# Reordering the start of a decoder step: x ahead of the constants, the first modulation's weights ahead of the projection's, TensorE's transposes of x spread

## The chip, the cores and the metric

The kernel runs on one core of one Trainium2 chip. A core has a matrix engine (TensorE, PE in the profile, with PEld for its weight loads), VectorE (DVE), ScalarE (ACT), GpSimd (POOL), and SyncE (SP), which here issues all transfers between device memory and the core's SBUF. Matmuls write into PSUM banks, from which DVE and ACT read. The metric is the device time of one execution in microseconds, the median of several runs.

## The reference, cut to what matters

One layer of a decoder for a prompt (512 tokens) and 8 x 8 sampled tokens, all in fp32. The part that the change concerns is the first three lines:

```
mod = einsum('bd,dn->bn', silu(c), w_ada) + b_ada
sh1, sc1, g1, sh2, sc2, g2 = split(mod, 6)
u = x * (1 + sc1) + sh1
proj = einsum('bsd,dn->bsn', u, w_in)      # 10752 columns: q, k, v, recurrence, gates
...                                        # attention, HGRN2 recurrence, branches, w_out,
...                                        # LayerNorm, squared-ReLU MLP, LayerNorm
```

c has 9 rows (one for the prompt, eight for the samples), x 576 rows of 1024. Only sh1 and sc1 are needed for u.

## The kernel before, in words

Everything lives with the model dimension on partitions: x is transposed on PE into eight tiles xT[k] of 128 x 576 (k counts the 128-wide slices of the 1024 columns), and u likewise. fp32 products are made of three passes of a faster type: each operand is cast to a high part on ACT (whi, uh) and the remainder is subtracted on DVE (wlo, ul), and a product is hi*hi + hi*lo + lo*hi. A projection block of 128 output columns over all k thus takes 8 x 3 matmuls for each half of the tokens.

Each engine works through its instructions in the order in which the Python code issues them; nothing is reordered at run time. Later in the kernel a planner (`Side`, with a cost model in `Engine`) mixes attention work between the projection's matmuls; the start, which the change concerns, is written out by hand, near the end of `decoder_step`.

The start has these parts:

- `x_load(e)` loads half e of x's columns as five tiles `xtm` (four of the prompt, one of the samples). `x_transposed(xtm, ks)` makes xT[k]: four transposes of 128 x 128 and one of 64 x 64 on PE into two PSUM banks tagged "tr", one copy on ACT, one on DVE.
- `ada_load(s)` loads the weights of modulation s (s = 0 to 3): eight tiles `wada`, 256 KB each. Set s holds the shift and the scale for k = 2s and 2s + 1.
- `ada(s, w)` is a generator in two halves. The first: eight matmuls (PE `tr<-wada,cT`, sixteen records in a trace) and a copy to SBUF on ACT (`moda`). The second: four transposes on PE (`tr<-ident,moda`), a reduction on DVE (`mt`), and an addition (`mod`). Each `next(shift[s])` runs one half.
- `make_u(k)` makes u for slice k: ACT writes uh for the prompt, POOL and ACT for the samples, DVE makes u and then the remainder ul.
- `load_one()` loads one slot of w_in: `wraw`, 1 MB, four slices of k and four blocks j. `split_slot(u0, j, slot)` makes whi and wlo of block j from it. Slot 0 serves k = 0 to 3, slot 1 k = 4 to 7.
- `early_mm(k)` makes the products of slice k for the first three blocks (`n_early`), each in two token halves, into the banks tagged lin, att and sx: 18 matmuls.

Before the change SP first issues ctile (the rows of c), ident (the identity), block_mask, vecs (all bias rows), then x's first half, slot 0 of w_in, two sets of modulation weights, x's second half, the third set, slot 1 of w_in, and the fourth set. PE transposes c and vecs, then x's columns 0 to 3, then runs the first modulation. After that, for each s: second half of modulation s, u for its two slices, the products of slice 2s - 1, those of slice 2s, the first half of modulation s + 1, and (for s = 0, 1) two more columns of x. In what follows "block 3" is the first projection block after this early stage; it is where the hand-written start ends.

Of the kernel before, what the change touches and what calls it, by code (L numbers as in the profile page):

```python
# [11 lines left out]
F32 = mybir.dt.float32  # L12
F32R = mybir.dt.float32r
U8 = mybir.dt.uint8
AF = mybir.ActivationFunctionType
OP = mybir.AluOpType
# [7 lines left out]
NS = NB * NTK  # L24
# [12 lines left out]
C_M0, C_M1, C_M2, C_SBC, C_SBN, C_BM, C_ID = 0, 256, 384, 512, 896, 1280, 1284  # L37
# [206 lines left out]
def decoder_step(ctx, tc, I, O):  # L244
# [21 lines left out]
    def page(shape, name, dtype=F32):  # L266
        return pages.tile(shape, dtype, name=name, tag="page")

    def bank(shape, tag, bufs=2):
        return psum.tile(shape, F32, name=tag, tag=tag, bufs=bufs)  # L270
# [9 lines left out]
    ident = consts.tile([128, 128], F32, name="ident")  # L280
    SP.dma_start(ident, I["cst"][:, C_ID:C_ID + 128])
    block_mask = consts.tile([128, 4], F32, name="block_mask")
    SP.dma_start(block_mask, I["cst"][:, C_BM:C_BM + 4])
    bias_of = {}
    vecs = page([128, 128], "vecs")
    SP.dma_start(vecs, I["rows"])
    lm = consts.tile([128, 8, 128], U8, name="lm")
# [89 lines left out]
    def split_slot(u, j, s):  # L377
        k0, kk, t = u["slots"][s]
        hi, lo = u["w"].setdefault(j, ([], []))
        for k in range(0, kk, 4):  # L380
            src = t[:, k:k + 4, j * 128:(j + 1) * 128]
            hi.append(page([128, 4, 128], "whi", F32R))
            lo.append(page([128, 4, 128], "wlo", F32R))
            A.activation(hi[-1], src, AF.Copy)
            V.tensor_sub(lo[-1], src, hi[-1])
# [88 lines left out]
    A.activation(csg, ctile, AF.Tanh, scale=0.5)  # L474
    V.scalar_tensor_tensor(csg, csg, 1.0, ctile, op0=OP.add, op1=OP.mult)
    V.tensor_scalar(csg, csg, 0.5, None, op0=OP.mult)
    pv = bank([128, 256], "tr")
    PE.transpose(pv[:, 128:200], csg, ident[:72, :72])
    PE.transpose(pv[:, 0:128], vecs, ident)
    V.tensor_copy(cT[:, :, 0:9], pv[:, 128:200].rearrange("p (k n) -> p k n", n=9))  # L480
    vT = consts.tile([128, 128], F32, name="vT")
    V.tensor_copy(vT, pv[:, 0:128])
    for part in (1, 4):
        V.tensor_scalar(vT[:, 8 * part:8 * part + 8], vT[:, 8 * part:8 * part + 8], 1.0, None, op0=OP.add)

    def vcol(off, k):
        return vT[:, off + k:off + k + 1]

    hnw = consts.tile([128, 1], F32, name="hnw")
    V.tensor_scalar(hnw, vcol(V_HN, 0), 0.5, None, op0=OP.mult)  # L490
    lbt = consts.tile([128, 4, 8], F32, name="lbt")
    lb0, lb1 = (vT[:, ROWS["lb_param"] + 8 * e:ROWS["lb_param"] + 8 * e + 8] for e in range(2))
    V.tensor_max(lbt[:, 0], lb0, lb1)
    V.tensor_sub(lbt[:, 1], lb0, lbt[:, 0])
    V.tensor_sub(lbt[:, 2], lb1, lbt[:, 0])
    A.activation(lbt[:, 1:3], lbt[:, 1:3], AF.Exp)
    V.tensor_add(lbt[:, 3], lbt[:, 1], lbt[:, 2])
    V.reciprocal(lbt[:, 3], lbt[:, 3])
    V.tensor_mul(lbt[:, 0], lbt[:, 1], lbt[:, 3])
    V.tensor_scalar(lbt[:, 1], lbt[:, 0], -0.5, 0.5, op0=OP.mult, op1=OP.add)  # L500
    V.tensor_scalar(lbt[:, 0], lbt[:, 0], 0.5, 0.5, op0=OP.mult, op1=OP.add)

    mod = consts.tile([128, 48, 9], F32, name="mod")

# [3 lines left out]
    def ada_load(s):  # L508

        wk = [page([128, 2, 256], "wada") for _ in range(KT)]  # L510
        for k in range(KT):
            src = I["w_ada"][0][k * 128:(k + 1) * 128, 0:2048].rearrange("p (a c) -> p a c", a=2)
            SP.dma_start(wk[k], src[:, :, s * 256:(s + 1) * 256])
        return [w.rearrange("p a c -> p (a c)") for w in wk]

    def ada(s, wk=None, u=None):

        if u:
            load_more()
            while not loaded(u):  # L520
                yield 0, 1000
                load_more()
            yield 0, tuple(t for _, _, t in u["slots"])
        pa = bank([128, 512], "sx" if u else "tr")
        for k in range(KT):
            PE.matmul(pa[32 * (k % 4):32 * (k % 4) + 32], cT[:, k], u["slots"][k // 4][2][:, k % 4] if u else wk[k],
                      start=(k < 4), stop=(k >= 4), skip_group_check=True)
        if u:
            weights_done(u["slots"])
        ma = page([128, 512], "moda")  # L530
        A.activation(ma, pa, AF.Copy)
        yield 1900, 2000.0
        pm = bank([128, 4, 128], "sx" if u else "tr")
        for jj in range(4):
            PE.transpose(pm[:, jj], ma[:, jj * 128:(jj + 1) * 128], ident)
        mt = tiny([128, 4, 9], "mt")
        V.tensor_reduce(mt, pm.rearrange("p j (q n) -> p j n q", q=4)[:, :, 0:9], axis=AX.X, op=OP.add)
        if u:
            m, b = mod[:, s * 4:s * 4 + 4], vT[:, s * 4:s * 4 + 4, None]
        else:  # L540
            m, b = (t.rearrange("p (a k) n -> p a k n", a=2)[:, :, 2 * s:2 * s + 2] for t in (mod[:, 0:16], vT[:, 0:16, None]))
            mt = mt.rearrange("p (a k) n -> p a k n", a=2)
        V.tensor_add(m, mt, b.to_broadcast(list(mt.shape)))
        if u and s in (4, 5):
            V.tensor_scalar(m, m, 0.5 / ALPHA, None, op0=OP.mult)
        yield 436, 0
# [961 lines left out]

    xT = []

    def x_load(e):
        ts = []
        for b in range(5):
            rows = 128 if b < 4 else NS
            t = page([128, 512], "xtm")
            src = I["x_prompt"][0, b * 128:(b + 1) * 128] if b < 4 else I["x_sample"].rearrange("b t d -> (b t) d")
            SP.dma_start(t[:rows], src[:, e * 512:(e + 1) * 512])
            ts.append(t)
        return ts

    def x_transposed(xtm, ks):
        for k in ks:
            c = slice(k * 128, (k + 1) * 128)
            t = page([128, NT], "xT")
            xT.append(t)
            xp = bank([128, 4, 128], "tr")
            for b in range(4):
                PE.transpose(xp[:, b], xtm[b][:, c], ident)
            A.activation(t[:, 0:NP], xp.rearrange("p a b -> p (a b)"), AF.Copy)
            xsp = bank([128, NS], "tr")  # L1530
            PE.transpose(xsp, xtm[4][0:64, c], ident[0:64, 0:64])
            V.tensor_copy(t[:, NP:NT], xsp)
# [6 lines left out]
    def ahead(i):  # L1539
        while i < len(flat):  # L1540
            u, j = flat[i]
            if "ada" in u:
                if id(u) not in done_split:
                    done_split.add(id(u))
                    side.add("a", ada(u["ada"], u=u))
                i += 1
                continue
            if (id(u), j) not in done_split and not (u["tok"] and j % 5):
                done_split.add((id(u), j))
                split(u, j)  # L1550
            return

    def make_u(k):

        t = page([128, NT], "u32")
        U_hi[k], U_lo[k] = page([128, NT], "uh", F32R), page([128, NT], "ul", F32R)
        x = xT[k]
        A.activation(U_hi[k][:, 0:NP], x[:, 0:NP], AF.Identity, scale=mcol(1, k), bias=mcol(0, k))
        G.tensor_mul(sm(t[:, NP:NT]), sm(x[:, NP:NT]), msam(1, k))
        G.tensor_add(sm(t[:, NP:NT]), sm(t[:, NP:NT]), msam(0, k))  # L1560
        V.tensor_scalar(t[:, 0:NP], x[:, 0:NP], mcol(1, k), mcol(0, k), op0=OP.mult, op1=OP.add)
        A.activation(U_hi[k][:, NP:NT], t[:, NP:NT], AF.Copy)
        V.tensor_sub(U_lo[k], t, U_hi[k])

    xs = [page([128, 4, 128], "xs", F32R) for _ in range(2)]

    xa = x_load(0)
    load_one()
    wa = [ada_load(0), ada_load(1)]
    xb = x_load(1)  # L1570
    wa.append(ada_load(2))
    load_one()
# [5 lines left out]
    n_early = 3  # L1578
    u0 = units[0]
    early = {}  # L1580

    def early_mm(k):
        for j in range(n_early):
            for h in range(2):
                if k == 0:
                    early[j, h] = bank([128, HF], ("lin", "att", "sx")[j])
                mm_part(u0["w"][j], 8, u_x, h, early[j, h], (k,))

    x_transposed(xa, range(4))
    for j in range(n_early):  # L1590
        done_split.add((id(u0), j))
        split_slot(u0, j, 0)
    shift = [ada(s, w) for s, w in enumerate(wa)]
    wa.clear()
    next(shift[0])
    for s in range(4):
        next(shift[s])
        for k in (2 * s, 2 * s + 1):
            make_u(k)
        if s == 3:  # L1600
            ahead(n_early)
        if s:
            early_mm(2 * s - 1)
        if s == 2:
            next(shift[3])
        early_mm(2 * s)
        if s < 2:
            next(shift[s + 1])
            x_transposed(xb, (2 * s, 2 * s + 1))
        if s == 1:  # L1610
            for j in range(n_early):
                split_slot(u0, j, 1)
    early_mm(KT - 1)
    shift.clear()
    for j in range(n_early):
# [729 lines left out]
```

## Time and profile before

| | us |
|---|---|
| median of 3 runs | 1359.46 (1358.33 to 1359.71) |
| the profiled execution | 1361.52 |
| its span, first to last instruction | 1359.7 |
| PE busy in the span | 1308.3 |
| first matmul of the first modulation | 16.65 |
| first product of the projection | 24.12 |
| block 3 begins | 59.73 |

A row of the profile names the engine, the operation, and the tiles as out<-in; a bracket behind it gives the idle time of the engine ahead of it and what ended that. The line is always L173, since a helper records every operation, so one reads by tiles. A granted clock of 1.00 is TensorE's full clock, 0.50 half of it. The record of the granted clock begins at 21.75 us; before that a view shows 1.00 for want of a record.

### The profile page before, as it was taken

The numbers are of one execution on the slowest core, as the hardware profiler recorded it, in microseconds if no ns is written. First come the engines' busy times: TensorE is split into PE (matmuls) and PEld (weight loads), VectorE is DVE, ScalarE is ACT, GpSimd is POOL, SyncE is SP. The second block draws the span as 40 slices with busy tenths as digits, with TensorE's granted clock in tenths as the row PEclk, the third lists the DMA queues.
The fourth block names the chain that finished last, engine by engine and source line by source line (L and its number), as shares of the span: only waits on it lengthen the run. The fifth ranks groups of instructions, "written<-read, shape, count | busy, mean of one in ns | idle before, by whom it ended". The sixth has DMA issues, their size and how long they took to land.

```text
span 1359.7 us, 24393 instructions
## 1 busy us (share of the span) xinstructions
PE 1308.3 (96%) x9480; PEld 1206.2 (89%) x9480; DVE 837.9 (62%) x1669; ACT 524.2 (39%) x1164; POOL 319.7 (24%) x367
## 2 busy tenths in 40 slices
PE   6999999999889899999999999999999999999996
PEld 3899899899878787788898999999899999999995
DVE  2446556557776886657555526656545744766867
ACT  2423323333332322333233423224555742753851
POOL 0332023016525673225234400000530000000004
PEclk9999999999999999999999999999999999999999
DMA  9789889789988887775545514241126352453522
GB/s 292 266 294 333 274 290 350 250 264 319 295 275 282 295 286 252 222 246 173 171 146 166 159 32 140 68 158 64 62 81 248 115 198 113 156 225 119 221 95 70
DMA packets 186824, 274.11 MB, mean 202 GB/s; under 512 B 16012, under 2 KB 92628, under 8 KB 186196
## 3 DMA queue, kind: packets, MB, share of 16 engines
q1 hardware_dynamic: 186708, 272.54, 59.7%
q8 instruction: 75, 1.23, 0.4%
q14 instruction: 41, 0.34, 0.1%
HBM read 212.81 MB, written 76.46 MB: 213 GB/s over the span
## 4 chain that ended last, share of the span: by engine, by line
PE 82%; DVE 7%; DMA 4%; ACT 3%; issue 2%; POOL 1%; SPq 0%; DVEq 0%; POOLq 0%; ACTq 0%
PE lin L173 60%; PE att L173 11%; PE sx L173 7%; PE tr L173 4%; DVE wlo L173 2%; DMA qb<-qsc 2%; DVE res L173 1%; DMA out_dram<-kv 1%; DMA sgl<-ssc 1%; ACT whi L173 1%; DVE sc L173 1%; DVE hf L173 0%; DMA xtm<-in_x_sample_dram 0%; DVE st L173 0%; SPq L173 0%
## 5 line engine op out<-in xcount | busy, mean ns | idle before, releaser
L173 DVE TENSOR_TENSOR wlo<-wraw,whi 128x512 fp32r<-128x512 f32 (+1 forms) x335 | 271.1, 847 | 107.5 <-ACT whi L173 104.5
L173 PE MATMUL lin<-uh,whi 128*128 128x288 f32 x992 | 298.5, 301 | 5.3 <-DVE hso L173 3.7
L173 PE MATMUL lin<-uh,wlo 128*128 128x288 f32 x992 | 298.8, 301 | 1.9 <-DVE wlo L173 1.9
L173 PE MATMUL lin<-ul,whi 128*128 128x288 f32 x992 | 299.0, 301 | 1.2 <-DVE ul L173 1.2
L173 ACT ACTIVATE whi<-wraw 128x512 fp32r<-128x512 f32 (+1 forms) x335 | 211.3, 681 | 111.2 <-PE lin L173 36.5
L173 PEld LDWEIGHTS lin<-ul,whi 128*128 128x128 f32 x992 | 187.7, 189 | 14.4 <-issue 11.6
L173 PEld LDWEIGHTS lin<-uh,whi 128*128 128x128 f32 x992 | 187.7, 189 | 11.2 <-DVE hso L173 4.2
L173 PEld LDWEIGHTS lin<-uh,wlo 128*128 128x128 f32 x992 | 187.7, 189 | 6.9 <-issue 3.8
L173 POOL TENSOR_TENSOR qb<-qb,kv 128x512 f32<-128x512 f32 x96 | 128.9, 1360 | 202.8 <-DMA qb<-qsc 69.6
L173 PE MATMUL lin<-hdl,whi 128*128 128x288 f32 (+1 forms) x448 | 133.3, 298 | 1.4 <-DVE hdl L173 1.4
L173 PE MATMUL lin<-hdh,whi 128*128 128x288 f32 (+1 forms) x448 | 134.1, 299 | 0.0
L173 PE MATMUL lin<-hdh,wlo 128*128 128x288 f32 (+1 forms) x448 | 133.2, 297 | 0.0
L173 POOL TENSOR_TENSOR res<-res,lgb 128x512 f32<-128x512 f32 (+2 forms) x10 | 14.8, 1484 | 335.8 <-ACT res L173 335.4
L173 PEld LDWEIGHTS lin<-hdl,whi 128*128 128x128 f32 x448 | 84.5, 189 | 1.7 <-DVE hdl L173 1.7
L173 PEld LDWEIGHTS lin<-hdh,whi 128*128 128x128 f32 x448 | 84.5, 189 | 0.0
L173 PEld LDWEIGHTS lin<-hdh,wlo 128*128 128x128 f32 x448 | 84.3, 188 | 0.0
L173 PE MATMUL lin<-whi,uh 128*128 128x512 f32 x160 | 69.6, 435 | 2.5 <-ACT whi L173 1.1
L173 PE MATMUL lin<-wlo,uh 128*128 128x512 f32 x160 | 64.8, 405 | 1.1 <-DVE wlo L173 1.1
L173 DVE TENSOR_REDUCE sc<-qb 128x4 f32<-128x512 f32 x96 | 63.6, 678 | 3.3 <-POOL qb L173 3.1
L173 PE MATMUL lin<-whi,ul 128*128 128x512 f32 x160 | 64.0, 400 | 0.0
L173 POOL TENSOR_TENSOR hk<-hk,T 128x256 f32<-128x256 f32 (+1 forms) x48 | 40.7, 847 | 71.7 <-PE att L173 43.2
L173 ACT ACTIVATE P<-P,stat_p 128x128 f32<-128x128 f32 (+1 forms) x48 | 20.1, 420 | 93.7 <-DVE stat_p L173 93.7
(427 smaller groups left out, 2893.5 us busy)
## 6 DMA issues: line engine op xcount, KB each, us to landing
wraw<-in_w_in_dram SPq DMA_DIRECT2D x42, 1024.0 KB
kv<-in_cache_kv_w_dram SPq DMA_DIRECT2D x144, 256.0 KB
qb<-qsc SPq DMA_DIRECT2D x96, 256.0 KB
wraw<-in_w_down_dram SPq DMA_DIRECT2D x18, 1024.0 KB
out_dram<-kv SPq DMA_DIRECT2D x64, 256.0 KB
wraw<-in_w_ada_dram SPq DMA_DIRECT2D x16, 1024.0 KB
wraw<-in_w_up_dram SPq DMA_DIRECT2D x16, 1024.0 KB
out_dram<-in_cache_kv_w_dram SPq DMA_DIRECT2D x32, 512.0 KB
```

The costliest lines, as they stand in the source:

```text
L173: return f(out, *args, **kw)
```

## The change

Four things move; no instruction's work changes.

1. On SP, block_mask and vecs go behind x's first half, and slot 0 of w_in goes behind the first set of modulation weights.
2. On PE, the transposes of x are spread: columns 0 and 1, then vecs, then the first half of modulation 0, then columns 2 and 3. The second half of x (columns 4 to 7) goes ahead of the first halves of modulations 2 and 3 instead of behind those of 1 and 2.
3. Six to twelve products of an odd slice are split off: some stand ahead of a modulation's second half, the rest behind it.
4. On ACT and DVE, the casts of slot 0 are issued between and behind `make_u(0)` and `make_u(1)`, the casts of slot 1 behind `make_u(4)` and `make_u(5)`, and the work on `lbt` (bounds of the recurrence's gate) goes from the very start into modulation 1.

The SP queue at its start, as a difference (- before, + now):

```order
 L173 DMA ctile<-in_c_rows_dram 72x128
 L173 DMA ident<-in_cst_dram 128x128
-L173 DMA block_mask<-in_cst_dram 128x4
-L173 DMA vecs<-in_rows_dram 128x128
 L173 DMA xtm<-in_x_prompt_dram 128x512 x4
 L173 DMA xtm<-in_x_sample_dram 64x512
-L173 DMA wraw<-in_w_in_dram 128x4x512
-L173 DMA wada<-in_w_ada_dram 128x2x256 x16
+L173 DMA vecs<-in_rows_dram 128x128
+L173 DMA wada<-in_w_ada_dram 128x2x256 x8
+L173 DMA wraw<-in_w_in_dram 128x4x512
+L173 DMA block_mask<-in_cst_dram 128x4
```

So x's five tiles are the third to seventh transfer instead of the fifth to ninth, and the first eight wada tiles no longer follow wraw.

On PE, modulation 1 of before, from its matmuls to the first product of the next slice:

```order
L173 MATMUL tr<-wada,cT 32x512 x8
L173 MATMUL tr<-ident,xtm 128x128 x4
L173 MATMUL tr<-ident,xtm 128x64
L173 MATMUL tr<-ident,xtm 128x128 x4
L173 MATMUL tr<-ident,xtm 128x64
L173 MATMUL tr<-ident,moda 128x128 x4
L173 MATMUL lin<-uh,whi 128x288
```

The same modulation now; the six sx products are the last of slice 1, and the lin product is the first of slice 2:

```order
L173 MATMUL tr<-wada,cT 32x512 x8
L173 MATMUL tr<-ident,moda 128x128 x4
L173 MATMUL sx<-uh,whi 128x288
L173 MATMUL sx<-ul,whi 128x288
L173 MATMUL sx<-uh,wlo 128x288
L173 MATMUL sx<-uh,whi 128x288
L173 MATMUL sx<-ul,whi 128x288
L173 MATMUL sx<-uh,wlo 128x288
L173 MATMUL lin<-uh,whi 128x288
```

The ten transposes of x have left the place between the two halves. In before the lin product shown belongs to slice 1, whose u was made earlier; all 18 products of slice 1 stand there.

On ACT, modulation 2 of before (the copy moda, x's columns 6 and 7, slot 1's casts, then u of slices 4 and 5):

```order
L173 ACTIVATE moda<-tr 128x512
L173 ACTIVATE xT<-tr 128x512 x2
L173 ACTIVATE whi<-wraw 128x512 x3
L173 ACTIVATE uh<-xT,mod 128x512
L173 ACTIVATE uh<-u_509 128x64
L173 ACTIVATE uh<-xT,mod 128x512
L173 ACTIVATE uh<-u_518 128x64
```

The same place now (xT is here columns 6 and 7 again):

```order
L173 ACTIVATE moda<-tr 128x512
L173 ACTIVATE uh<-xT,mod 128x512
L173 ACTIVATE uh<-u_484 128x64
L173 ACTIVATE uh<-xT,mod 128x512
L173 ACTIVATE uh<-u_493 128x64
L173 ACTIVATE whi<-wraw 128x512 x3
L173 ACTIVATE xT<-tr 128x512 x2
```

Slot 1's three casts stand behind both slices' u instead of ahead of them. The diff's core:

```diff
-    SP.dma_start(block_mask, I["cst"][:, C_BM:C_BM + 4])
...
+    xa = x_load(0)
     vecs = page([128, 128], "vecs")
     SP.dma_start(vecs, I["rows"])
...
-    xa = x_load(0)
+    wa = [ada_load(0)]
     load_one()
-    wa = [ada_load(0), ada_load(1)]
+    SP.dma_start(block_mask, I["cst"][:, C_BM:C_BM + 4])
+    wa.append(ada_load(1))
     xb = x_load(1)
...
-    def early_mm(k):
-        for j in range(n_early):
+    def early_mm(k, js=range(n_early)):
+        for j in js:
...
-    x_transposed(xa, range(4))
+    shift = [ada(s, w) for s, w in enumerate(wa)]
+    wa.clear()
+    x_transposed(xa, (0, 1))
+    vectors()
+    next(shift[0])
+    x_transposed(xa, (2, 3))
+    next(shift[0])
     for j in range(n_early):
         done_split.add((id(u0), j))
+        if j < 2:
+            make_u(j)
         split_slot(u0, j, 0)
-    shift = [ada(s, w) for s, w in enumerate(wa)]
-    wa.clear()
-    next(shift[0])
-    for s in range(4):
-        next(shift[s])
-        for k in (2 * s, 2 * s + 1):
-            make_u(k)
-        if s == 3:
-            ahead(n_early)
-        if s:
-            early_mm(2 * s - 1)
-        if s == 2:
-            next(shift[3])
-        early_mm(2 * s)
-        if s < 2:
-            next(shift[s + 1])
-            x_transposed(xb, (2 * s, 2 * s + 1))
-        if s == 1:
-            for j in range(n_early):
-                split_slot(u0, j, 1)
+    early_mm(0)
+    early_mm(1, (0, 1))
+    next(shift[1])
+    gate_bounds()
+    next(shift[1])
+    make_u(2)
+    make_u(3)
+    early_mm(1, (2,))
+    early_mm(2)
+    x_transposed(xb, (0, 1))
+    next(shift[2])
+    early_mm(3, (0,))
+    next(shift[2])
+    make_u(4)
+    make_u(5)
+    for j in range(n_early):
+        split_slot(u0, j, 1)
+    early_mm(3, (1, 2))
+    early_mm(4)
+    x_transposed(xb, (2, 3))
+    next(shift[3])
+    early_mm(5, (0,))
+    next(shift[3])
+    make_u(6)
+    make_u(7)
+    ahead(n_early)
+    early_mm(5, (1, 2))
+    early_mm(6)
     early_mm(KT - 1)
```

`vectors()` is the transpose of vecs with its copy and two additions, `gate_bounds()` the work on hnw and lbt; both stood inline at the start, vecs' transpose sharing a bank with c's.

More of the change, by code (lines that the diff above doesn't have):

```diff
@@ L282, in decoder_step, with x_load @@
     block_mask = consts.tile([128, 4], F32, name="block_mask")
-    SP.dma_start(block_mask, I["cst"][:, C_BM:C_BM + 4])
     bias_of = {}
+    def x_load(e):
+        ts = []
+        for b in range(5):
+            rows = 128 if b < 4 else NS
+            t = page([128, 512], "xtm")
+            src = I["x_prompt"][0, b * 128:(b + 1) * 128] if b < 4 else I["x_sample"].rearrange("b t d -> (b t) d")
+            SP.dma_start(t[:rows], src[:, e * 512:(e + 1) * 512])
+            ts.append(t)
+        return ts
+    xa = x_load(0)
     vecs = page([128, 128], "vecs")
@@ L476, in decoder_step @@
     V.tensor_scalar(csg, csg, 0.5, None, op0=OP.mult)
[L477 to L480, printed above, removed]
+    pv = bank([128, 128], "tr")
+    PE.transpose(pv[:, 0:72], csg, ident[:72, :72])
+    V.tensor_copy(cT[:, :, 0:9], pv[:, 0:72].rearrange("p (k n) -> p k n", n=9))
     vT = consts.tile([128, 128], F32, name="vT")
-    V.tensor_copy(vT, pv[:, 0:128])
@@ L483, in decoder_step @@
-    for part in (1, 4):
-        V.tensor_scalar(vT[:, 8 * part:8 * part + 8], vT[:, 8 * part:8 * part + 8], 1.0, None, op0=OP.add)
+    hnw = consts.tile([128, 1], F32, name="hnw")
+    lbt = consts.tile([128, 4, 8], F32, name="lbt")
     def vcol(off, k):
         return vT[:, off + k:off + k + 1]
[L489 to L501, printed above, removed]
+    def vectors():
+        pv = bank([128, 128], "tr")
+        PE.transpose(pv, vecs, ident)
+        V.tensor_copy(vT, pv)
+        for part in (1, 4):
+            V.tensor_scalar(vT[:, 8 * part:8 * part + 8], vT[:, 8 * part:8 * part + 8], 1.0, None, op0=OP.add)
@@ new lines, in gate_bounds @@
+    def gate_bounds():
+        V.tensor_scalar(hnw, vcol(V_HN, 0), 0.5, None, op0=OP.mult)
+        lb0, lb1 = (vT[:, ROWS["lb_param"] + 8 * e:ROWS["lb_param"] + 8 * e + 8] for e in range(2))
+        V.tensor_max(lbt[:, 0], lb0, lb1)
+        V.tensor_sub(lbt[:, 1], lb0, lbt[:, 0])
+        V.tensor_sub(lbt[:, 2], lb1, lbt[:, 0])
+        A.activation(lbt[:, 1:3], lbt[:, 1:3], AF.Exp)
+        V.tensor_add(lbt[:, 3], lbt[:, 1], lbt[:, 2])
+        V.reciprocal(lbt[:, 3], lbt[:, 3])
+        V.tensor_mul(lbt[:, 0], lbt[:, 1], lbt[:, 3])
+        V.tensor_scalar(lbt[:, 1], lbt[:, 0], -0.5, 0.5, op0=OP.mult, op1=OP.add)
+        V.tensor_scalar(lbt[:, 0], lbt[:, 0], 0.5, 0.5, op0=OP.mult, op1=OP.add)
@@ L1509, in decoder_step @@
     xT = []
[L1511 to L1519, printed above, removed]
     def x_transposed(xtm, ks):
```

## The prediction

> **What bounds the kernel now.** I read the page first. TensorE (PE) is busy for nearly the whole span, so the time moves when PE stands idle or runs at half clock.
>
> ```profile
> PE 1308.3 (96%) x9480; PEld 1206.2 (89%) x9480; DVE 837.9 (62%) x1669; ACT 524.2 (39%) x1164; POOL 319.7 (24%) x367
> ```
>
> The edit touches only the start, so next I asked for the stretches of the start: up to the first modulation's matmuls, those, its second half and the first products, the rest of the early stage, and the block after it. Columns: stretch, its length, busy us of PE, PEld, DVE, ACT, POOL with counts, granted clock, DMA share, GB/s.
>
> ```profile
> 0.00:16.65 16.65, 7.33 (x23) 3.98 (x23) 3.33 (x19) 4.23 (x8) 1.55 (x15) 1.00 0.78 241
> 16.65:21.92 5.27, 4.58 (x16) 1.08 (x17) 1.90 (x3) 2.13 (x4) 0.00 (x0) 1.00 1.10 348
> 21.92:29.08 7.16, 5.03 (x22) 4.43 (x23) 3.10 (x6) 1.97 (x4) 1.81 (x4) 0.76 1.08 331
> 29.08:59.73 30.65, 28.35 (x209) 21.87 (x209) 13.25 (x27) 14.56 (x31) 10.48 (x28) 1.00 0.78 262
> 59.73:69.70 9.97, 9.97 (x66) 9.86 (x66) 2.50 (x4) 4.12 (x12) 0.00 (x0) 1.00 0.81 275
> ```
>
> PE idles 9.3 us before 16.65 and only 2.3 us from 29.08 to 59.73. There is much to win ahead of 22 us and little after 29 us. The chain of waits around the end of the stage gives the unit prices:
>
> ```profile
> 47.03 1.85 PE tr L173 x16
> 51.53 0.45 PE tr L173 x4
> 58.93 0.80 PE sx L173 x6
> 59.73 9.28 PE lin L173 x60
> ```
>
> A modulation's first half (eight matmuls, sixteen records) is 1.9 us, its four transposes 0.45, six products 0.80 (0.133 each), so a block of k (18 products) 2.4. The early stage ends at 59.73, and I forecast where that point goes: the same instructions follow it, in the same order on PE.
>
> **The first modulation (gain).** The timeline up to it, with x's loads, its last tile, the transposes of one column of x, and the last weights:
>
> ```profile
> 1.65 0.43 SPq L173 DMA_DIRECT2D block_mask<-in_cst_dram  x1
> 2.59 1.85 SPq L173 DMA_DIRECT2D xtm<-in_x_prompt_dram  x4
> 10.76 0.34 PE L173 MATMUL tr<-ident,xtm 64*128 64x64 f32 x1 [0.18 <-DMA xtm<-in_x_sample_dram]
> 14.88 1.41 PE L173 MATMUL tr<-ident,xtm 128*128 128x128 f32 x5 [0.32 <-DVE xT L173]
> 16.65 3.83 PE L173 MATMUL tr<-wada,cT 128*32 128x512 f32 x15 [0.36 <-issue]
> 19.32 0.18 PEld L173 LDWEIGHTS tr<-wada,cT 128*32 128x32 f32 x2 [0.57 <-DMA wada<-in_w_ada_dram]
> 21.27 0.60 ACT L173 ACTIVATE moda<-tr 128x512 f32<-128x512 f32 x1 [3.09 <-PE tr L173]
> 21.92 0.66 PE L173 MATMUL tr<-ident,moda 128*128 128x128 f32 x4 [0.69 <-ACT moda L173]
> ```
>
> The constants leave the queue ahead of x, which starts at 1.65 instead of 2.59: 0.9 us. The 1 MB of w_in leaves the way of the weights: 1.05 MB at 348 GB/s is 3.0 us. The last weights, wanted at 19.32, come at 15.4, and the matmuls end 1.95 later, at 17.3. Two columns of x now stand between them and the transposes of the result, each 1.77 (14.88 to 16.65) at the slow clock: the second half (T0) starts at 20.8 instead of 21.92. Of 3.9 us 1.1 is left. Bounds: with no earlier arrival T0 stays at 21.9. With x at 348 GB/s from 2.6 (1.18 MB, 3.4 us), then 2.1 MB (6.0), 1.95 and 3.5, T0 is 17.5.
>
> **From T0 to the second modulation (cost).** A second half is a chain over four engines; the second one of before, and the casts of one 1 MB slot of w_in with their remainders, which before ran under the first modulation:
>
> ```profile
> 32.39 0.86 PE L173 MATMUL tr<-ident,xtm 128*128 128x128 f32 x5 [0.32 <-DVE xT L173]
> 33.57 0.66 PE L173 MATMUL tr<-ident,moda 128*128 128x128 f32 x4 [0.32 <-DVE xT L173]
> 34.26 0.31 DVE L173 TENSOR_REDUCE mt<-tr 128x36 f32<-128x144 f32 x1 [0.75 <-PE tr L173]
> 34.88 0.82 ACT L173 ACTIVATE uh<-xT,mod 128x512 fp32r<-128x512 f32 x1 [1.20 <-DVE mod L173]
> 36.24 0.76 DVE L173 TENSOR_TENSOR ul<-u,uh 128x576 fp32r<-128x576 f32 x1 [0.85 <-ACT uh L173]
> 37.05 0.40 PE L173 MATMUL lin<-ul,whi 128*128 128x288 f32 x1 [0.31 <-DVE ul L173]
> 37.19 0.26 ACT L173 ACTIVATE uh<-u 128x64 fp32r<-128x64 f32 x1 [0.27 <-POOL u L173]
> 37.55 0.76 DVE L173 TENSOR_TENSOR ul<-u,uh 128x576 fp32r<-128x576 f32 x1
> ```
>
> ```profile
> 16.52 1.66 ACT L173 ACTIVATE whi<-wraw 128x512 fp32r<-128x512 f32 x3
> 17.18 1.90 DVE L173 TENSOR_TENSOR wlo<-wraw,whi 128x512 fp32r<-128x512 f32 x3 [0.63 <-ACT whi L173]
> ```
>
> Counted from T (33.57): mt 0.7, uh done 2.13, PE can use ul at 3.48; the second k's uh is complete at 3.88, its ul at 4.74. The three remainders of slot 0 (0.63 each) now stand on DVE between and behind these: the first product with the last of them cannot run before T0 + 4.74 + 1.9 = T0 + 6.6. Then 4 products at half clock (0.24) and 12, nearly all at full clock: the second modulation's matmuls start at T0 + 9.3 = 30.1, against 29.08. By then 12 products (1.6 us) more are done.
>
> **The stretch to the end of the stage (cost).** Before, transposes of x and a whole block of 18 products filled each chain. Now:
> - Second modulation: matmuls to 32.0. Nothing stands between them and their own transposes, so PE waits for moda, 0.7 as at 21.92: T1 = 32.7. The gate bounds moved in front of mt, and ACT's exp stands behind moda. Their rows:
>
> ```profile
> 5.81 0.22 ACT L173 ACTIVATE lbt<-lbt 128x16 f32<-128x16 f32 x1 [2.95 <-DVE lbt L173]
> 6.70 0.38 DVE L173 TENSOR_SCALAR lbt<-lbt 128x8 f32<-128x8 f32 x2
> ```
>
>   From 5.81 to 7.08 is 1.27, against the 0.7 that mt waits anyway: 0.55 late. Beside the chain PE has its transposes (0.45) and six products (0.8), idle until uh at T1 + 2.13 + 0.55 = 35.4 (1.4 idle) and, after one product, until ul at 36.75 (1.2 idle). The other 17 end at 39.0.
> - Two columns of x, 1.18 each (32.39 to 33.57): 41.4. Third modulation 1.9, six products 0.8 (these do cover moda): T2 = 44.1. Transposes 0.45 and twelve products 1.6: PE is through at 46.15. The next block needs slot 1's casts, which the new order puts behind both k's of u on ACT: T2 + 3.88 + 0.62 = 48.6, idle 2.5 us; its remainder comes behind ul on DVE at T2 + 4.74 + 0.69 = 49.55, idle 0.8. Sixteen products: 51.7.
> - Two columns 2.4, fourth modulation 1.9, six products 0.8: T3 = 56.8. Twelve products end at 58.85; ul comes at T3 + 3.48 = 60.3, idle 1.2. 17 products and the last block, 2.3 + 2.4: **65.0 against 59.73, +5.3 us.**
>
> The transfers are not late: after 15.4 three sets of weights (2.1 MB each), two slots of w_in and x's second half are 9.6 MB, 27.5 us at 348 GB/s. The fourth set is in by 43, and PE asks at 54.
>
> **The clock.** Stretches of 3.4 us along its steps; the last two are from elsewhere in the trace:
>
> ```profile
> 11.51:14.92 3.41, 2.78 (x11) 1.74 (x11) 0.45 (x2) 1.19 (x2) 0.00 (x0) 1.00 1.08 356
> 21.75:25.16 3.41, 1.11 (x6) 0.67 (x6) 2.00 (x5) 1.83 (x4) 1.77 (x4) 1.00 1.09 359
> 25.16:28.57 3.41, 3.41 (x14) 3.41 (x15) 1.10 (x2) 0.26 (x1) 0.04 (x1) 0.50 1.08 312
> 462.07:465.48 3.41, 1.69 (x12) 1.40 (x11) 3.41 (x4) 0.00 (x0) 3.41 (x4) 1.00 0.44 154
> 465.48:468.90 3.42, 2.40 (x17) 2.35 (x17) 1.69 (x5) 2.32 (x11) 1.40 (x1) 1.00 0.61 188
> ```
>
> A stretch with PE a third busy was followed by one at 0.50; one half busy was not. PE now has 0.13 us of work between 46.15 and 49.55: unless the boundary halves that gap, half clock follows, where 14 products fill 3.41 us (0.24 each) instead of 1.9. About ten products meet it: 1.1 us. The gaps at 34.0 to 36.75 can bring another. I take one: +5.3 + 1.1 = **+6.4**. The Trainium skill, "TensorE: Matmul & The Clock Gate", section "HAM oscillation — how this bites in real kernels", asks only for no idle gap of over about 3.4 us; by that rule nothing here throttles, and the sum would be +5.3, 1364.8. The trace disagrees: 21.75 to 25.16 held matmuls and was followed by half clock.
>
> The profiled execution took 1361.52 us, its span 1359.7 and 1.8 around it, 2.06 above the median of the runs. I expect 1367.9 of a profiled run and **1365.9** of the median. Of this kernel 0.2% (2.7 us) can be told from no change.
>
> **Rivals.**
> - *Faster:* the early weights pay. The modulation's matmuls run straight into transposes of x, the clock is full there, each column costs 1.18: T0 = 19.7. Products at full speed from then on (T0 + 6.6 + 2.1 = 28.4), and idle time after that as small as before (30.65 less the 1.6 done): the stage ends at 57.4, 2.3 us early, or 4 with T0 near 18: 1355.5 to 1357.2. For it: 9.3 us of idle ahead of 16.65. It decides if casts and u are ready when PE comes; the order on ACT and DVE speaks against that. 7%.
> - *Same:* the delay is taken up. Behind the stage the chain leaves PE:
>
> ```profile
> 75.08 3.45 DMA qb<-qsc
> 78.56 0.63 ACT whi L173
> 81.69 2.39 DVE wlo L173 x2
> 84.13 18.69 PE lin L173 x101
> ```
>
>   If these transfers came when they come now, 3.5 to 5 us would vanish: 1361 to 1362.4. Against it: qsc is written from the first products, so it moves with them. An early x (T0 = 17.5) with no cold stretch ends alike: 17.5 + 9.3 and 34.9 from there on (30.1 to 65.0) is 61.7, +2.0, 1361.5; with all its products at full clock 1360.8. 13%.
> - *Slower still:* three cold stretches. For it: 11.51 to 14.92 was 2.78 us busy, all transposes of x, and the matmuls from 16.65 on still ran slow (fifteen records in 3.83 us, sixteen in 1.85 at 47.03; waits for weights are in it). If transposes do not hold the clock, the two pairs of columns (2.4 us each), with gaps beside them, bring it down too: three times 1.1 instead of once, 1368.1, and up to 1369.5 with T0 at 21.9. Against it: from 29.08 to 59.73 there were two such pairs, and the clock stayed at 1.00. The Trainium skill states on the same page, section "Part 4: PE-mode transpose", that a transpose does not count as PE-busy in the same way. By that rule this rival holds. 12%.
> - *x no earlier:* its tiles wait for something else, T0 21.9, +7.5: 1367.0. It lies in the forecast's own case.
>
> **How the numbers follow.** The forecast's case has 68%. The range 1360.8 to 1369.5 reaches from T0 = 17.5 without a cold stretch to T0 = 21.9 with three, and leaves out the faster rival and a tail on both sides. Faster 0.07, same 0.13, slower 0.80.
>
> **What would show it.** Right: the matmuls with wada start near 13 and end near 17; T0 near 21; PE idle about 2.5 us ahead of the first product with slot 1's casts, released by ACT whi; block 3 starts near 65. Wrong: PE idle of 3 us or less between the second modulation and block 3, or that block before 60.

## The result, and the profile after

| | before | after |
|---|---|---|
| median, same chip, four runs each (us) | 1358.91 | 1369.45 |
| ratio, 95% interval | | 1.006 [1.0031, 1.0088] |
| the profiled execution (us) | 1361.52 | 1369.54 |
| its span (us) | 1359.7 | 1367.8 |
| block 3 begins (us) | 59.73 | 66.76 |

The changed kernel is slower by 0.6%. (A ratio in this document is the one on record with its interval, not the quotient of the two medians, which is 1.0078 here.) The forecast was 1365.9 with a range to 1369.5; the direction holds, the measured median lies at the upper end. The page of the changed kernel has for the engines:

```profile
PE 1311.7 (96%) x9480; PEld 1210.0 (88%) x9480; DVE 838.8 (61%) x1669; ACT 523.1 (38%) x1164; POOL 319.9 (23%) x367
```

The same 9480 instructions are 3.4 us more busy, although none was added: some of them ran slower. The stretches of the changed kernel's start, cut at the same points of the program as before's (columns as there; the record of the clock begins at 15.38 us here, so the 1.00 of the first row, and of the second up to there, stands for want of a record):

```profile
0.00:11.72 11.72, 4.41 (x12) 2.16 (x12) 1.19 (x5) 2.79 (x4) 1.54 (x15) 1.00 0.78 246
11.72:18.63 6.91, 6.18 (x27) 2.24 (x26) 0.98 (x5) 1.67 (x3) 0.00 (x0) 1.00 1.07 360
18.63:29.59 10.96, 8.28 (x34) 7.25 (x34) 5.32 (x13) 3.53 (x8) 1.81 (x4) 0.69 1.09 344
29.59:66.76 37.17, 30.12 (x197) 23.14 (x197) 14.03 (x32) 14.95 (x32) 10.21 (x28) 0.91 0.57 192
66.76:76.73 9.97, 9.97 (x67) 9.87 (x66) 2.50 (x4) 4.13 (x12) 0.00 (x0) 1.00 0.80 271
```

The first modulation starts 4.9 us earlier (11.72 against 16.65), and its second half 3.3 us earlier (18.63 against 21.92). Then the kernel loses: at the second modulation it is 0.5 us behind (29.59 against 29.08), and the last early stretch takes 37.17 us instead of 30.65, PE idle for 7.05 of it instead of 2.3. Its clock was 1.00 before; now it is 0.91. Block 3 itself takes 9.97 us in both.

The chain of waits of the changed kernel, around block 3 and behind it:

```profile
66.76 9.28 PE lin L173 x60
...
82.11 3.45 DMA qb<-qsc
...
91.00 18.69 PE lin L173 x101
```

Block 3 is 7.03 us late, the transfer of qb behind it as well (82.11 against 75.08), and the products behind that 6.87. The transfer did not take up the delay. At the end of the span 8.1 us are lost, so 7.0 of them are lost ahead of block 3.

The timeline of the changed kernel, PE's rows that stood at a wait or that the prediction placed:

```profile
11.72 4.46 PE L173 MATMUL tr<-wada,cT 128*32 128x512 f32 x16
14.93 0.18 PEld L173 LDWEIGHTS tr<-wada,cT 128*32 128x32 f32 x2 [0.53 <-DMA wada<-in_w_ada_dram]
18.63 0.66 PE L173 MATMUL tr<-ident,moda 128*128 128x128 f32 x4 [0.32 <-DVE xT L173]
21.54 0.40 PE L173 MATMUL lin<-uh,whi 128*128 128x288 f32 x1 [2.25 <-ACT whi L173]
29.59 1.92 PE L173 MATMUL tr<-wada,cT 128*32 128x512 f32 x16
32.31 0.66 PE L173 MATMUL tr<-ident,moda 128*128 128x128 f32 x4 [0.80 <-ACT moda L173]
34.81 0.40 PE L173 MATMUL lin<-uh,whi 128*128 128x288 f32 x1 [1.04 <-ACT uh L173]
36.10 0.61 PE L173 MATMUL lin<-ul,whi 128*128 128x288 f32 x1 [0.90 <-DVE ul L173]
42.17 1.92 PE L173 MATMUL tr<-wada,cT 128*32 128x512 f32 x16 [0.32 <-DVE xT L173]
49.09 0.40 PE L173 MATMUL lin<-uh,whi 128*128 128x288 f32 x1 [1.97 <-ACT whi L173]
50.05 0.61 PE L173 MATMUL lin<-uh,wlo 128*128 128x288 f32 x1 [0.43 <-DVE wlo L173]
61.83 0.40 PE L173 MATMUL lin<-ul,whi 128*128 128x288 f32 x1 [0.65 <-DVE ul L173]
```

Each wait that the new order was expected to make is there, at its place and with its releaser: moda 0.80, uh 1.04, ul 0.90, slot 1's whi 1.97 and wlo 0.43, ul 0.65.

The rest is the clock. Stretches of 3.4 us of the changed kernel, laid on its changes of clock:

```profile
18.78:22.20 3.42, 1.17 (x6) 0.64 (x5) 2.26 (x5) 2.23 (x5) 1.81 (x4) 1.00 1.10 350
22.20:25.61 3.41, 2.99 (x12) 2.63 (x12) 3.06 (x9) 1.18 (x3) 0.00 (x0) 0.50 1.07 354
25.61:29.03 3.42, 3.42 (x16) 3.42 (x16) 0.00 (x0) 0.00 (x0) 0.00 (x0) 0.50 1.09 328
32.44:35.86 3.42, 1.73 (x11) 1.28 (x11) 2.37 (x9) 1.67 (x3) 1.71 (x4) 1.00 1.06 370
35.86:39.27 3.41, 3.17 (x13) 3.17 (x14) 1.41 (x3) 0.36 (x2) 0.34 (x1) 0.50 1.09 349
46.10:49.51 3.41, 1.45 (x10) 1.09 (x8) 2.72 (x6) 3.02 (x7) 1.81 (x4) 1.00 0.47 172
49.51:52.92 3.41, 2.98 (x13) 2.87 (x13) 1.69 (x3) 0.57 (x2) 0.00 (x0) 0.50 0.01 2
```

Four stretches ahead of block 3 ran at half clock, against one on record in before (25.16 to 28.57). Ahead of each spell lies a stretch in which PE was busy for 1.17 to 1.73 us of 3.4, that is, one of the chains in which it waited. So two theories stood after the result. One: the waits cost the time, and the half clock fills time that would be idle anyway. The other: the waits and the half clock cost about as much each. The experiments part them.

### The profile page after: what moved, and what is told of

Its sections match the earlier page's. It is cut to its first block, busy times and chain, and to the rows that moved or that the text cites. A ratio compares the mean times of both kernels' runs of the same rounds, so it can differ in the third digit from the quotient of the medians.

```text
span 1367.8 us, 24395 instructions
## 1 busy us (share of the span) xinstructions
PE 1311.7 (96%) x9480; PEld 1210.0 (88%) x9480; DVE 838.8 (61%) x1669; ACT 523.1 (38%) x1164; POOL 319.9 (23%) x367
## 4 chain that ended last, share of the span: by engine, by line
PE 78%; DVE 8%; DMA 7%; ACT 3%; issue 2%; POOL 1%; SPq 0%; DVEq 0%; POOLq 0%; ACTq 0%
PE lin L173 58%; PE att L173 10%; PE sx L173 7%; PE tr L173 3%; DVE wlo L173 2%; DMA out_dram<-kv 2%; DMA wada<-in_w_ada_dram 2%; DMA wraw<-in_w_in_dram 1%; DVE res L173 1%; ACT whi L173 1%; DMA qb<-qsc 1%; DMA sgl<-ssc 1%; DVE sc L173 0%; ACT P L173 0%; DVE st L173 0%
```

## The experiments

Most experiments concern a point at 60 us of 1360, so block 3's start is the figure to compare; the whole time is given where it was measured, against runs of before on the same chip (medians 1360.89, 1361.2 and 1361.26 us on three chips). Two controls say how far each figure can be trusted.

**The controls.** Both kernels again, on one chip, as they are.

> The kernel before, once more with a profile, to see what varies by itself. Theory (the start is fixed but for the clock's phase, the rest of the variation lies in stages with transfers): block 3 within 1.6 us of 59.73, and the shift against the first profile of before is set between there and 520 us. Rival (the start varies as much as the change moved it): block 3 off by 3 us or more.

> The changed kernel once more, with a profile and timed, on this chip. Theory: block 3 between 64.3 and 66.8 (two or three half-clock stretches by the phase of the clock's windows), and 5 to 7 us later than in the profile of before on the same chip; the time 5 to 10 us over before. Rival: block 3 within 3 us of before's, and the first comparison's difference lay elsewhere.

Before again: 1363.69 us (one run), block 3 at 59.85, so 0.12 from the first, though its clock differed: half from 23.29 to 30.12 us instead of 25.16 to 28.57. After again: 1366.53 (12 runs), ratio 1.0044 [1.0028, 1.006]. Its profiled execution took 1365.08, and the chain has block 3 at:

```profile
65.69 9.28 PE lin L173 x60
```

That is 5.96 behind before's first trace instead of 7.03. The windows of the repeated changed kernel show the difference: two stretches at half clock instead of four.

```profile
17.68:21.10 3.42, 2.42 (x15) 1.50 (x14) 0.68 (x3) 1.78 (x3) 0.00 (x0) 1.00 1.10 349
21.10:24.51 3.41, 1.12 (x5) 0.82 (x6) 2.75 (x6) 3.00 (x7) 1.81 (x4) 1.00 1.08 366
24.51:27.92 3.41, 2.92 (x13) 2.57 (x12) 2.34 (x7) 0.41 (x1) 0.00 (x0) 0.50 1.08 318
...
48.40:51.82 3.42, 3.04 (x13) 2.80 (x12) 1.77 (x3) 0.65 (x2) 0.00 (x0) 0.50 0.06 24
```

The bounds of the stretches lie elsewhere (24.51 instead of 22.20), and so do the gaps in them: the wait around 34 us that was followed by half clock in the first trace was not in this one. T0, where the second half of the first modulation begins, lies at 20.18 us here instead of 18.63. Block 3 of one and the same kernel lay 1.07 us apart in one pair of executions and 0.12 in the other, so a difference of 1 us between two single traces shows little.

**The two halves of the change.** First the new start (loads, early weights, casts) with before's order from the second modulation on; then the old start with the new order.

```diff
     early_mm(0)
-    early_mm(1, (0, 1))
     next(shift[1])
-    gate_bounds()
-    next(shift[1])
+    x_transposed(xb, (0, 1))
+    for s in range(1, 4):
+        next(shift[s])
...
```

(The gate bounds stand behind the two columns of x of s = 1.) The old start with the new rest, its gate bounds at the very start again, as a difference from the changed kernel and cut:

```diff
-    xa = x_load(0)
     vecs = page([128, 128], "vecs")
...
-    wa = [ada_load(0)]
+    xa = x_load(0)
     load_one()
-    SP.dma_start(block_mask, I["cst"][:, C_BM:C_BM + 4])
-    wa.append(ada_load(1))
+    wa = [ada_load(0), ada_load(1)]
...
+    x_transposed(xa, range(4))
+    for j in range(n_early):
+        split_slot(u0, j, 0)
```

> The changed kernel up to and with the first block of products (new loads, x spread around modulation 0, slot 0's casts between u's), then the order of before for modulations 1 to 3 (columns of x between the halves, whole blocks of 18 beside each chain, slot 1's casts ahead of modulation 2). Theory (the new start gains, the new rest loses): the first block ends at 27.0 to 28 as in the changed kernel's trace with its 18 products, where before it ended at 29.08; 30.65 us from there on as before: block 3 begins near 57.7 to 58.7, time 1 to 2 us under before, 1357 to 1358. Rival (the new start gains nothing, since the modulation is only moved against casts and half clock): block 3 at 59.7 or later, time 1359 or over.

> The other half: loads and start of before (with the gate bounds where they were) up to modulation 0's u, then the changed kernel's order for everything after it. Theory (the loss is in the rest): block 3 begins 0 to 2 us later than in the changed kernel, 66.5 to 68.5, time about 8 us over before, 1366 to 1368; with the second experiment's gain of 1 to 2 the two halves add up to the change's +7 at block 3. Rival (the loss is in the new loads or in casts of slot 0): block 3 under 63.

Block 3 in the chain of the kernel with the new start, and of the one with the new rest:

```profile
58.46 9.28 PE lin L173 x60
```

```profile
68.12 9.27 PE lin L173 x60
```

Against 59.73 the new start gains 1.27 and the new rest costs 8.39; together 7.12, and the change has 7.03. The halves add up; that they do so to 0.1 is partly luck, since the clock alone moves block 3 by up to 1 us. In the whole time only the loss is seen: 1361.31 (10 runs), ratio 1.001 [0.9988, 1.0033], where 1357 to 1358 was expected, and 1372.4 (4 runs), ratio 1.0101 [1.0044, 1.0159], where 1366 to 1368 was. The chain of the kernel with the new start holds a transfer (kv, 6.92 us from 86.22 on) that the chain of before doesn't have there; whether that takes up the gain was not tried.

**Slot 1's casts ahead of the third modulation.** One piece of the new order alone is undone.

```diff
     x_transposed(xb, (0, 1))
+    for j in range(n_early):
+        split_slot(u0, j, 1)
     next(shift[2])
     early_mm(3, (0,))
     next(shift[2])
     make_u(4)
     make_u(5)
-    for j in range(n_early):
-        split_slot(u0, j, 1)
     early_mm(3, (1, 2))
```

> The changed kernel with one thing undone: slot 1's casts (whi, wlo) go back ahead of modulation 2, behind the transposes of columns 4 and 5; all else as changed. Theory (the stage lost time where casts stand behind u, and where the gaps bring half clock): the first product of slice 4 no longer waits for ACT whi (49.09 in the changed kernel) but for uh, near 47.1, and the rest of its block for ul at 48.1 instead of wlo at 50.05: 1.9 us. The gap shrinks to under a third of a 3.4 us stretch, so the half clock at 49.5 goes: 12 products at 0.13 instead of 0.24, another 1.4. Block 3 begins near 63.4 instead of 66.76, and the time is about 3.3 us under the changed kernel's, 1366. Rival (the whole stretch is held by the transfers or by ul, and the casts only stand beside it): block 3 within 0.7 us of 66.76.

The chain, and PE's rows at that place:

```profile
64.07 9.27 PE lin L173 x60
```

```profile
48.49 0.40 PE L173 MATMUL lin<-ul,whi 128*128 128x288 f32 x1 [0.65 <-DVE ul L173]
```

The wait for whi (1.97) and that for wlo (0.43) are gone, the one for ul (0.65) has come in, and no half clock follows. Block 3 is 2.69 earlier than after's (63.4 was expected, 64.07 measured). The whole time is 1365.12 (10 runs), ratio 1.0036 [1.0012, 1.006]: still slower than before. But two things went at once here, the gap and the half clock behind it.

**The gap filled, not closed.** The next two leave every instruction of the change where it is, and put work whose result is never read into the third gap (behind the transposes of the third modulation): nine matmuls of the identity with itself, or eighteen transposes of a tile of x.

```diff
     early_mm(3, (1, 2))
+    fill = bank([128, 128], "tr")
+    for _ in range(9):
+        PE.matmul(fill, ident, ident, start=True, stop=True)
 # or:   for _ in range(18): PE.transpose(fill, xb[0][:, 0:128], ident)
     early_mm(4)
```

> The changed kernel with nine fp32 matmuls of ident by ident into a bank that nobody reads, in the gap of modulation 2 between the last product of slice 3 (46.96) and the first of slice 4 (49.09). Theory (half clock follows an idle stretch): the stretch from 46.1 is now busy, the clock stays at 1.00 from 49.5 to 52.9, and the 12 products there run at 0.13 apart instead of 0.24: block 3 1.2 to 1.5 us earlier, near 65.4, though PE has more to do. Rival (the clock falls by time or by load, not for idle): clock 0.50 there again, block 3 at 66.8 or later.

> As the fourth experiment, but the same gap of modulation 2 is filled with 18 transposes of an x tile (2 us) instead of nine fp32 matmuls. The Trainium skill, page TensorE: Matmul & The Clock Gate, Part 4, states that a transpose does not count as PE-busy in the same way. If so, half clock follows the gap again as in the changed kernel: the 12 products run 0.24 apart, block 3 near 66.8 (less whatever an earlier half-clock stretch at 36 adds or spares). If PE's occupation counts, whatever it does, the clock stays at 1.00 behind the gap and block 3 begins near 64.3 to 65.4.

The timeline of the one with matmuls, around the filler:

```profile
45.73 2.17 PE L173 MATMUL tr<-ident 128*128 128x128 f32 x18
47.85 0.40 PE L173 MATMUL lin<-uh,whi 128*128 128x288 f32 x1
...
48.81 0.40 PE L173 MATMUL lin<-uh,wlo 128*128 128x288 f32 x1 [0.43 <-DVE wlo L173]
49.05 0.29 PE L173 MATMUL lin<-uh,whi 128*128 128x288 f32 x1
49.18 0.30 PE L173 MATMUL lin<-ul,whi 128*128 128x288 f32 x1
```

The casts come no sooner (wlo is waited for as before), but the products now follow each other at 0.13 us. Block 3 is at 64.24, 2.5 earlier than in the first after, in a kernel that does more work. The expectation was 65.4; the half clock at 36 us was missing too, as in after again, where nothing was filled, so only part of the 2.5 belongs to the filler. Its own share is seen from T2 on, where the transposes of the third modulation begin: from there to block 3 it is 20.57 us, against 21.84 and 21.81 in the two traces of the changed kernel, so 1.25, as expected (1.2 to 1.5). One run took 1364.38. With transposes block 3 is at 63.81 (one run, 1367.18), 20.56 behind T2, and its windows answer the other question, whether transposes hold the clock (the record begins at 16.95):

```profile
16.95:20.36 3.41, 2.59 (x15) 1.53 (x14) 0.51 (x3) 1.79 (x3) 0.00 (x0) 1.00 1.10 348
20.36:23.77 3.41, 0.95 (x4) 0.65 (x5) 2.79 (x6) 2.83 (x7) 1.81 (x4) 1.00 1.09 358
23.77:27.19 3.42, 3.10 (x13) 2.75 (x13) 2.47 (x8) 0.59 (x2) 0.00 (x0) 0.50 1.08 307
...
44.22:47.63 3.41, 3.40 (x29) 3.17 (x28) 2.69 (x6) 2.81 (x6) 1.81 (x4) 1.00 1.06 383
47.63:51.04 3.41, 2.99 (x22) 2.69 (x21) 1.91 (x4) 0.79 (x2) 0.00 (x0) 1.00 0.25 91
```

The stretch from 16.95 holds almost nothing but transposes (2.59 us), and the next stayed at full clock; so did the one behind 44.22, of which 2.1 us were filler transposes. The stretch from 20.36, with a gap and PE busy for 0.95, was followed by half clock. Here transposes hold the clock as matmuls do, and gaps lose it. Whether transposes alone would bring the clock up from half is not shown by any run.

**All gaps filled, the order kept.** This is the run that parts the two costs: fillers in three gaps, so that the clock should stay at 1.00 and the waits alone are left; then the same with slot 1's casts ahead as well.

```diff
     next(shift[0])
+    filler(9)          # 9 matmuls of ident with ident, never read
...
     early_mm(1, (2,))
+    filler(4)
     early_mm(2)
...
     early_mm(3, (1, 2))
+    filler(9)          # 4 with the casts ahead
     early_mm(4)
```

> The changed kernel with unread matmuls of ident with ident in three of its gaps: nine behind the transposes of modulation 0, four behind those products of slice 1 that follow modulation 1, nine behind those of slice 3. Every instruction of the change stays where it is. Theory (the lost time is waits of the new order plus half clock, and the two can be parted): the clock stays at 1.00 from 17 us to block 3; products come 0.13 apart from the first on; block 3 then shows the waits alone. From the run with the third gap filled (64.24) about 2 us more are saved, since its products from 22.7 to 27.9 ran at half clock: block 3 at 62.2, 2.5 behind before. Rival (waits alone set the end; the clock only fills them): block 3 stays at 64 or later. Second rival (clock alone): block 3 at 60 or earlier.

> As the kernel with all gaps filled, and besides it slot 1's casts stand ahead of the third modulation, as in the run with the casts ahead; the third filler is four matmuls instead of nine. Theory: the two repairs add, since one holds the clock and the other takes away the wait for whi: 62.2 less about 1.5, block 3 at 60.8, still 1 us behind before, because a product that waits for ul at every modulation is left (three waits of 0.7 us each). Rival: both repairs cured the same thing (the half clock at 49.5), block 3 no earlier than the kernel with all gaps filled. Second rival: the order itself is no worse than before's once these two are gone: block 3 at 59 or earlier, with x and the weights early.

The windows of the first from the record's start to block 3, and both chains:

```profile
15.77:61.86 46.09, 39.74 (x285) 31.16 (x285) 19.80 (x47) 20.16 (x42) 12.05 (x32) 1.00 0.78 258
```

```profile
61.86 9.28 PE lin L173 x60
```

```profile
60.25 9.28 PE lin L173 x60
```

With the clock at 1.00 all the way, block 3 stands at 61.86 (62.2 expected) and with the casts ahead at 60.25 (60.8 expected), so 1.61 hang on the place of slot 1's casts. From T0 to block 3 the kernel with its gaps filled took 43.42 us, the changed kernel 48.13 in its first trace and 45.51 in the repeat: half clock behind the gaps cost 4.7 us in one execution and 2.1 in the other. (The 4.90 from 66.76 to 61.86 hold 0.2 of an earlier T0 besides.) The 2.13 that are left against before are the balance of three things: the waits of the new order, its earlier start, and the half clock of before itself, which the filled kernel is spared. The last is some 1.5 us by an estimate from rows: 14 records in 25.16 to 28.57, at 0.24 instead of 0.13. So in the first pair of traces about 3.2 of the 7.03 us are clock, and about 3.8 waits less the gain of the early start. The theory that the half clock only fills idle time has fallen, and the one that clock alone counts as well. The whole times, ratio 1.0008 [0.9988, 1.0027] (1363.7, 10 runs) and 1.0003 [0.9987, 1.002] (1360.95, 12 runs), cannot be told from before's.

**A version that uses it.** The new start with before's rest, nine filler matmuls in the first gap, and slot 0's first two casts ahead of the modulation's second half, their remainders behind the first u's ul. From the first products on it is the kernel of the new start with the old rest.

```diff
     x_transposed(xa, (2, 3))
+    hi_part(0)                 # whi of blocks 0 and 1
+    hi_part(1)
     next(shift[0])
-    for j in range(n_early):
-        done_split.add((id(u0), j))
-        if j < 2:
-            make_u(j)
-        split_slot(u0, j, 0)
+    fill = bank([128, 128], "tr")
+    for _ in range(9):
+        PE.matmul(fill, ident, ident, start=True, stop=True)
+    make_u(0)
+    lo_part(0)                 # wlo
+    lo_part(1)
+    hi_part(2)
+    lo_part(2)
+    make_u(1)
     early_mm(0)
...
```

> The second experiment's kernel with two more edits: nine fp32 matmuls of ident by ident, which nobody reads, fill the gap between modulation 0's transposes and the first product, and slot 0's casts for blocks 0 and 1 go ahead of u, its remainders right behind the first u's ul. Theory (waits for casts, and half clock after gaps, are what the start costs): the clock stays at 1.00 from 20.7 on, the first product comes near 20.0 instead of 20.75, the first block ends near 23.7 instead of 26.35, and block 3 begins near 56 instead of 58.46 (before: 59.73); the time is 2 to 4 us under before. Rival (the loads of modulation 1 are late by then, or half clock comes all the same): block 3 at 57.8 or later, time as before.

The timeline at the filler and at the second modulation, and the chain:

```profile
19.43 2.17 PE L173 MATMUL tr<-ident 128*128 128x128 f32 x18
...
25.14 1.92 PE L173 MATMUL tr<-wada,cT 128*32 128x512 f32 x16
```

```profile
56.66 9.28 PE lin L173 x60
```

The clock stays at 1.00, the second modulation starts 3.94 us ahead of before's, block 3 3.07 (near 56 was expected). The first product, expected near 20.0, came at 21.36, right behind the filler; what a shorter filler would do was not tried. The whole time is 1358.12 (12 runs) against 1361.2, ratio 0.9971 [0.9957, 0.9985]: faster than both kernels (after again took 1366.53 on that chip). By the interval 2.0 to 5.9 us are gained. Its chain too leaves PE between 75 and 95 us for a transfer that the chain of before does not have there; what that costs was not measured.

```profile
84.46 6.82 DMA kv<-in_cache_kv_w_dram
```

## Why the prediction was right, and where its sizes were not

The stage from the transposes of modulation 0 (T0) to block 3 is a chain of pieces, T1 to T3 being the transposes of the later modulations. The prediction gave each a length; beside it what the changed kernel took and what it took with its gaps filled (us):

| piece | predicted | after | after, gaps filled |
|---|---|---|---|
| start to T0 | 20.8 | 18.63 | 18.44 |
| T0 to the second modulation | 9.3 | 10.96 | 8.94 |
| to T1 | 2.6 | 2.72 | 2.71 |
| to the third modulation | 8.7 | 9.86 | 8.46 |
| to T2 | 2.7 | 2.75 | 2.74 |
| to the fourth modulation | 10.0 | 10.93 | 9.68 |
| to T3 | 2.7 | 2.76 | 2.75 |
| to block 3 | 8.2 | 8.15 | 8.14 |
| sum | 65.0 | 66.76 | 61.86 |

1. **The waits: right.** At full clock each piece from T0 on is within 0.4 us of its forecast, 43.42 in all against 44.2. From T1 on the gaps and releasers are those named: slot 1's whi behind both u's, 2.5 forecast and 1.97 measured; moda 0.7 and 0.80; uh 1.4 and 1.04; ul 1.2 and 0.90, then 1.2 and 0.65; wlo 0.8 and 0.43. The longest wait of all, 2.25 for slot 0's whi ahead of the first product, was not named; the prediction reckoned that place by slot 0's last remainder, with its product at T0 + 6.6, and with the gaps filled this product came 6.71 behind T0 (25.15).
2. **T0: mis-sized by 2.2.** The step that failed is "Two columns of x now stand between them and the transposes of the result, each 1.77 ... at the slow clock". The two columns took 16.11 to 18.63, or 1.26 each, near the price at full clock (1.18), and from the end of the modulation's matmuls to T0 it was 2.45 us in both traces (16.18 to 18.63, in the repeat 17.72 to 20.18) instead of 3.5. That is 1.1. The rival "faster" had said so, with T0 at 19.7. The other 1.1 is the end of the matmuls, 16.2 instead of 17.3, the last weights having come at 14.93 instead of 15.4; in the repeat the matmuls ended at 17.7, so this part belongs to the execution. In the nine traces with the new loads T0 lies between 17.84 and 20.18.
3. **The clock: mis-sized by 3.6, the other way.** The step that failed is "I take one". The prediction gave one stretch of half clock 1.1, and the one behind slot 1's casts cost 1.25; but there were three spells instead of one. The pieces that hold products behind a gap took 2.02, 1.40 and 1.25 longer than with the gaps filled, 4.67 together. Behind T0 only four products had been put at half clock; there it cost most, since it stayed for two stretches (22.20 to 29.03). In the repeat there were two spells, of one stretch each, and they cost 2.1: this term is not the same in two executions.
4. **The sum: right by two errors.** The forecast for block 3 was 65.0 + 1.1 = 66.1, and it came at 66.76; 2.2 too late at T0 and 0.8 in the other waits stand against 3.6 too little for the clock. That 7.0 came so near to 6.4 is thus partly chance. The top of the range is 0.3 more than its terms give: three cold stretches at 1368.1 and T0 later by 1.1 are 1369.2, not 1369.5, and the measured median of 1369.45 lies between the two.
5. **From block 3 to the end.** The profiled pair is 8.0 us apart, 7.0 of it at block 3. The medians are 10.5 apart, since the profiled before ran 2.6 above its median this time; after again gave 0.44%, about 6 us. The forecast of 0.47% lies within both intervals. Behind block 3 two executions of one kernel differ by 2 (before) and 3.4 us (after); what makes them differ was not tried.
6. **The rivals.** *Same* needed the transfer to stay; it moved by 7.03. *Faster* needed "idle time after that as small as before"; with the waits in place it was not. Where the old rest, a filled gap and slot 0's casts moved ahead provide it, block 3 stands at 56.66, and the rival's price was 57.4. *Slower still* named more half clock and was right on that, but for a reason that fell: it said that transposes do not hold the clock. In most stretches they do: the one at 16.95 held 2.59 us of them and nothing was lost behind it, so the rule of the Trainium skill ("TensorE: Matmul & The Clock Gate", section "Part 4: PE-mode transpose") that a transpose does not count as PE-busy in the same way did not hold there as far as holding the clock goes (one stretch that went the other way is told below). By the other rule (same page, "HAM oscillation — how this bites in real kernels") nothing here should have throttled. It did, behind gaps of 1.97 and 2.25 us, and behind a stretch with gaps of 0.80 and 1.04.

## What to carry to other kernels

Where a reordering opens a gap of 2 us on TensorE, the gap is only part of the price: the stretch behind it may run at half clock, and here that cost 4.7 us in one execution and 2.1 in another, of a delay of 7.0 and 6.0. Look in the profile for short stretches with PE less than half busy, and close them, or fill them with matmuls that nobody reads. A chain over four engines could be costed piece by piece from one profile, here to within half a microsecond a piece; the state of the clock behind each gap has to be costed as well, for every gap.

## What the runs showed of the hardware that was not expected

- **The granted clock changes in steps of 3.41 us, and their phase is not the program's.** Records of half clock ahead of block 3 lasted 3.41 or 6.83 us; they began at 22.20 in one execution of the changed kernel and at 24.51 in another. The Trainium skill, "TensorE: Matmul & The Clock Gate", section "Part 1: The HAM clock gate (the "warmup" mystery)", gives a free-running window of 3413 ns; the traces agree.
- **The bound is not settled.** In the rows shown, half clock followed full-clock stretches with PE busy for 0.95 to 1.73 us of 3.41. It followed none with 2.42 or more, nor the 1.69 at 462 us of before. Two stretches speak against a bound between 1.7 and 2: in the kernel with one gap filled by matmuls, 2.19 us, all of them transposes, had half clock behind them, and in the one filled with transposes so had 2.21 us, all of them products of the projection. So the first is no sign that transposes count for less. On the other side 1.55 us in the repeat of before (453.37) kept the full clock. The profile models the ends of matmuls, so its busy time may not be what the chip goes by.

```profile
17.65:21.06 3.41, 2.19 (x14) 1.31 (x12) 0.95 (x4) 1.54 (x3) 0.00 (x0) 1.00 1.10 349
21.06:24.47 3.41, 1.65 (x5) 1.33 (x6) 2.73 (x5) 3.32 (x7) 1.81 (x4) 0.50 1.08 365
```

```profile
85.21:88.63 3.42, 2.21 (x7) 1.70 (x7) 3.42 (x4) 1.84 (x4) 1.53 (x2) 1.00 1.04 407
88.63:92.04 3.41, 3.41 (x9) 2.65 (x9) 2.10 (x4) 1.38 (x3) 0.00 (x0) 0.50 0.98 327
```

- **Coming back takes a nearly full stretch.** At half clock, 2.99 us busy (22.20 in the changed kernel) kept it down for another 3.41, and so did 3.15 (20.70 in the kernel with the new start and the old rest); 2.92 (24.51 in the repeat) and 2.98 (49.51) did not. So this bound, too, is not one number of busy time as the profile counts it.
